# Masks added on VectorE, 1 / rms spread over the columns through HBM in three stages, FoX values in thirds, and squares of the embedding moved to later places

## Chip, cores, metric

The kernel runs on one core of a Trainium2 chip. The metric is the device time of one execution in microseconds (us), taken as a median of several executions. TensorE (PE) multiplies matrices into PSUM; VectorE (DVE), ScalarE (ACT) and GpSimd (POOL) do the elementwise work; SyncE (SP) issues most transfers. DVE and ACT can read PSUM. Each engine has its own stream of instructions, done in order.

## Reference

The reference is a trunk of two layers with 256 tokens of 1024 elements, all in float32. Cut to what matters:

```python
for i in range(2):
    x = x + 0.5 * swiglu(rms_norm(x, g), w_in, w_out)     # FFN, hidden size 2816
    x = x + mixer(rms_norm(x, g))                         # layer 0: MLA, layer 1: FoX
    x = x + 0.5 * swiglu(rms_norm(x, g), w_in, w_out)     # FFN
    x = x + gated embedding of p[i], gate from rms_norm(x, g)
out = rms_norm(x, g)

def attention:                                            # 8 heads, blocks of 128 queries
    s = where(allowed, scores, -1e30)
    o = softmax(s) @ v
# MLA: allowed = key's chunk of 64 <= query's chunk
# FoX: allowed = key <= query, and s += cum[query] - cum[key]; its projection gives q, k, v and 8 gates
```

The layers' order, and with it the names used below: FFN 0, MLA, FFN 1, embedding 0, FFN 2, FoX, FFN 3, embedding 1.

## The kernel before

**Precision and weights.** Every large product takes float32 as two parts, high and low, and does three matmuls: high by high, high by low, low by high. Activations lie with features on the 128 partitions and tokens on 256 columns (a token has 1024 features, so 8 blocks, `KD`), each block as a pair; one matmul against high weights takes both parts of a block at once (512 columns, L236), a second one against low weights takes the high part (256 columns, L237). The class `Weights` (L63 to 139) runs a plan of all weight tiles in order of use. A fetch on SP's queue brings a tile of 512 KB into `raw` (four buffers, L90), ACT copies it rounded into `whi` (L99), and DVE subtracts to get `wlo` (L103); there are seven buffers of such pairs. `pump` does the next tile's DVE step and issues the next fetch, `get` takes tiles for use, and `catch_up` pumps when fewer than some number lie ahead.

**Order.** The order in the code is the order on each engine: there is no scheduler. PSUM has seven banks in rotation and an eighth for small tiles.

**Norms.** The class `Norm` (L262 to 320) collects what the next stage needs while this one ends: `high` writes the gain times x, rounded (ACT at L276, or DVE at L274), `low` the rest (DVE, L281), `square` a square on ACT (L287), which POOL adds to `acc` (L292). The division by the rms is done behind the next stage's product: `by_token` (L301 to 311) sums `acc` over partitions by two matmuls into `pst`, DVE makes the mean `v` (L309), and POOL the power −1/2, `rtok`, with a token on each partition, 128x2 (L311). `by_column` (L313 to 320) spreads it to 256 columns on every partition: two matmuls with `rtok` broadcast against the identity (four records, L316) and an ACT copy, `rb` (L319).

**FFN** (L323 to 414). Each of 22 chunks of the hidden layer has a gate bank `pg` and an up bank `pu`. A bank ends as `two` = bank times `rb` (DVE, L330), `gu` (POOL), a sigmoid-weighted product over ACT and POOL, and `hs`, the split result (ACT L213, DVE L217). The first pair of banks (`blocks`, L253) is begun without the last feature block, so that this block's `high` and `low` may come late: first blocks 0 to 6 of every bank, then block 7. Then comes chunk 1's gate with `by_token`, and its up with `by_column`.

**Attention** (L417 to 556). For a head, `scores` (L424) has TensorE fill `psc`, where one bank holds 128 queries by 128 keys and 128 queries by 256 keys; the mask comes in as a matmul of the identity against a table of 0 and a very negative number (`masked`, L558 to 564, 8 in MLA, 8 in FoX); DVE reduces the two maxima (L428, L429) and makes the bias `nm` (L432 or L438); ACT takes the exponential of `psc` with its sum `den` (L441, L442). `shares` divides, TensorE turns the shares into `pt` (L456), ACT copies them to `ptS` (L458), and `po` is the product with the values (L463, L464). Weight products of later heads and of the output lie between these as fillers.

**FoX values** (L746 to 775). The projection to 1024 value columns and 8 gate columns runs in four chunks: 264, 256, 256 and 256 columns, each with 8 blocks, 2 halves of the tokens and 3 matmuls (L221 to L223), `pv`. `by_token` stands in chunk 0, `by_column` in chunk 1.

**Embedding 0** (`ple`, L814 to 855). For each of 8 feature blocks d: product `ps`, `zg` = `ps` times `rb` (DVE, L818), sigmoid `sg` (ACT, L819), `low` of block d − 1, a pump, `ge` = embedding times `sg` (L827), `state` += `ge` (L828), then `high` and `square` of block d for FFN 2's norm.

**Start** (L964 to 996). The first weights and x come as eight pieces (`lead0`, `lead1`) on SP's queue; TensorE does 18 matmuls on zeros (`cold`, L983) until the first piece is there.

Of the kernel before, what the change touches and what calls it, by code (L numbers as in the profile page):

```python
# [11 lines left out]
F32 = mybir.dt.float32  # L12
# [7 lines left out]
P = 128  # L20
# [20 lines left out]
GAINS = 80  # L41

# [100 lines left out]
def trunk(ctx, tc, xT, xt, pT, pos, freq, bf, lead0, lead1, ffn_in, ffn_out, w_down, w_uq, w_ukv, mla_o,  # L143
          fox_qk, fox_v, fox_f, fox_o, ple_gate, ple_proj, ple_rows, gain_row, out):
# [6 lines left out]
    psum = ctx.enter_context(tc.tile_pool(name="psum", bufs=7, space=bass.MemoryType.PSUM))  # L151
    psm = ctx.enter_context(tc.tile_pool(name="psm", bufs=1, space=bass.MemoryType.PSUM))
# [23 lines left out]
    plan.extend(fox_f[c] for c in range(2))  # L176
    plan.extend(fox_v[c] for c in range(KD - 2))
# [4 lines left out]
    plan.extend(ple_rows[c, k] for c in range(2) for k in range(KD // 2))  # L182

# [69 lines left out]
    def blocks(ps, x):  # L253

        ws = W.get(len(ps))
        for ks in (range(KD - 1), range(KD - 1, KD)):
            for p, w in zip(ps, ws):
                part(p, w, x, ks, KD - 1)
        W.done(*ws)


    class Norm:  # L262
# [50 lines left out]
        def by_column(self):  # L313
            pb = psm.tile([P, T], F32, name="pb", tag="small")
            for t in range(2):
                nc.tensor.matmul(pb[:, t * P:(t + 1) * P], self.rtok[:, t:t + 1].to_broadcast([P, P]), ident,  # L316
                                 start=True, stop=True)
            self.rb = work.tile([P, T], F32, name="rb", bufs=3)
            nc.scalar.activation(self.rb, pb, AF.Copy)  # L319
            self.rb2 = self.rb.rearrange("p (o t) -> p o t", o=1).to_broadcast([P, 2, T])  # L320


    def ffn(norm, nxt, then=None, first=None, meanwhile=None, later=None):  # L323
# [35 lines left out]
        if first:  # L359
            waits.append((bank("pg"), bank("pu")))  # L360
            first([p for ps in waits for p in ps])
        else:
            blocks(waits[0], norm.pair)
            W.pump(2)
        at = len(waits)
        for c in range(at, KF):
            pg = bank("pg")
            block(pg, norm.pair)
            if c == at:
                if not first:  # L370
# [12 lines left out]
            up(c, pu, c > at)  # L383
# [33 lines left out]
    def attention(project, score, v, scale, nxt, lag, fills, early, cumq=None):  # L417
# [6 lines left out]
        def scores(h):  # L424
            ps = bank("psc", (P, 3 * P))
            score(h, (ps[:, :P], ps[:, P:]), ps.rearrange("p (a b) -> p a b", b=P)[:, 0::2, :])
            m = work.tile([P, 2], F32, name="m", bufs=3)
            nc.vector.reduce_max(m[:, 0:1], ps[:, :P], axis=AX.X)  # L428
            nc.vector.reduce_max(m[:, 1:2], ps[:, P:], axis=AX.X)  # L429
            nm = work.tile([P, 2], F32, name="nm", bufs=3)  # L430
            if cumq is None:
                nc.vector.scalar_tensor_tensor(nm, m, -1.0, scale, op0=ALU.mult, op1=ALU.mult)  # L432
# [6 lines left out]
            pr = work.tile([P, 3 * P], F32, name="pr", bufs=4)  # L439
            den = work.tile([P, 2], F32, name="den", bufs=3)  # L440
            nc.scalar.activation(pr[:, :P], ps[:, :P], AF.Exp, bias=nm[:, 0:1], scale=by[0], accum_out=den[:, 0:1])  # L441
            nc.scalar.activation(pr[:, P:], ps[:, P:], AF.Exp, bias=nm[:, 1:2], scale=by[1], accum_out=den[:, 1:2])  # L442
            probs[h] = pr, den
# [113 lines left out]

    def masked(diagonal, i):  # L558


        a = slice(0 if i else P // 2, P)
        n = a.stop - a.start
        nc.tensor.matmul(diagonal[:, :, a], identb, cmask[:, i:i + 1, a].to_broadcast([P, 2, n]), start=False,
                         stop=False)
# [7 lines left out]
    def mla(norm, nxt):  # L572
# [111 lines left out]
        def score(h, dst, diagonal):  # L684
            for t in range(2):
                nc.tensor.matmul(dst[t], qT[:, h, t * P:(t + 1) * P], kT[:, h, :(t + 1) * P], start=t == 0, stop=False)
            masked(diagonal, 0)
            for t in range(2):
                nc.tensor.matmul(dst[t], qr[:, h, t * P:(t + 1) * P], kr[:, h % 2, :(t + 1) * P], start=False,
                                 stop=t == 1)  # L690

        attention(project, score, v, qscale, nxt, 3, MLA_FILLS, 4)


    def fox(norm, nxt):
# [50 lines left out]
        for c in range(4):  # L746
            w = W.get(2)
            n = T + H if c == 0 else T
            pv = [bank("pv0", (P, n)), bank("pv1", (P, n))]
            for k in range(KD):  # L750
                for t in range(2):
                    a = (k % 4) * n
                    mm3(pv[t], [norm.pair[:, k, u, t * P:(t + 1) * P] for u in range(2)],
                        [u[:, a:a + n] for u in w[k // 4][1:]], k == 0, k == KD - 1)
                if (c, k) == (0, KD - 2):
                    norm.by_token()
                elif (c, k) == (1, 3):
                    norm.by_column()
                elif (c, k) == (2, 2):
                    steps = gates()  # L760
                if steps:
                    next(steps, None)
                if k % 4 == 3:
                    W.done(w[k // 4])
                    if k == 3:
                        W.pump()
                        W.catch_up()
            for t in range(2):
                r = norm.rtok[:, t:t + 1]
                if c == 0:  # L770
                    nc.scalar.activation(zt[:, t, :].rearrange("p (j i) -> p j i", i=32)[:, :, :H],
                                         pv[t][:, T:].rearrange("p (o h) -> p o h", o=1).to_broadcast([P, 3, H]),
                                         AF.Copy, scale=r)
                nc.scalar.activation(v[:, t, c * T:(c + 1) * T], pv[t][:, :T], AF.Copy, scale=r)
            W.pump()
# [12 lines left out]
        def score(h, dst, diagonal):  # L788
# [3 lines left out]
            masked(diagonal, 1)  # L792
# [4 lines left out]
        attention(project, score, v, FOX_SCALE, nxt, 2, FOX_FILLS, 4, cumq=cumq)  # L797
# [16 lines left out]
    def ple(pp, norm, nxt):  # L814
        def gated(d, z, e):
# [4 lines left out]
            if d:  # L820
                nxt.low(d - 1, hT[:, d - 1, :])
# [141 lines left out]

    ROW = T + 4 * P  # L964
    lead = big.tile([P, 2 * KD + KD * ROW + 2 * D], F32, name="lead", tag="big")
# [3 lines left out]
    nc.sync.dma_start(lead[:, :2 * KD + ROW], lead0)  # L969
# [12 lines left out]
    for _ in range(18):  # L982
        nc.tensor.matmul(cold, warm[:, :P], warm, start=True, stop=True)  # L983
# [39 lines left out]
    identb = const.tile([P, P], BF16, name="identb")  # L1023
    cmask = const.tile([P, 2, P], BF16, name="cmask")
# [7 lines left out]
    def tables():  # L1032
# [6 lines left out]
        nc.vector.tensor_copy(identb, ident)  # L1039
        yield  # L1040
        nc.gpsimd.memset(cmask, 0.0)
        nc.gpsimd.memset(cmask[:64, 0, 64:], NEG)
        nc.gpsimd.affine_select(out=cmask[:, 1, :], in_=cmask[:, 1, :], compare_op=ALU.is_ge, fill=NEG, base=0,
# [94 lines left out]
    for i in range(2):  # L1138
# [8 lines left out]
        if i == 0:  # L1147
            n0, n1 = Norm(G_FFN + 16, KD, D), Norm(G_MIX + 8, KD, D)
            ple(p.pair, n3, n0)
            ffn(n0, n1, AF.Exp)  # L1150
        else:
            ple_by_token(p.pair, n3)
# [8 lines left out]
def _layout(x, p, positions, ffn_norm, ffn_w_in, ffn_w_out, mix_norm, mla_w_down, mla_q_norm, mla_w_uq,  # L1161
# [41 lines left out]

    v = w[:, 2 * hd + T:3 * hd].reshape(2, KD // 2, P, 3, T)
    a["fox_v"] = np.ascontiguousarray(v.transpose(3, 0, 2, 1, 4)).reshape(KD - 2, P, D)
    f = np.concatenate([w[:, 2 * hd:2 * hd + T], w[:, 3 * hd:]], axis=1).reshape(2, KD // 2, P, T + H)
    a["fox_f"] = np.ascontiguousarray(f.transpose(0, 2, 1, 3)).reshape(2, P, -1)
# [11 lines left out]
          "fox_qk", "fox_v", "fox_f", "fox_o", "ple_gate", "ple_proj",  # L1219
# [21 lines left out]
```

## Time and profile before

| | us |
|---|---|
| median of 3 runs | 999.35 (998.24 to 999.6) |
| the profiled execution | 998.72 |
| its span | 996.9 |
| busy: DVE, ACT, POOL | 740.9, 514.8, 422.7 |
| granted TensorE clock | 0.998 |

The profile takes one execution; its span runs from the first to the last recorded instruction. Records of TensorE overlap, since matmuls are pipelined, so that what a matmul costs is read from one start to the next. A row of the timeline has its start, its duration, the engine, the line, the operation, its tiles and shapes, and, in brackets, the idle time of the engine before it with what ended it. A row of the groups has the busy time of all, the mean of one in ns, and the idle time before them.

### The profile page before, as it was taken

How to read it: one execution, taken by the hardware profiler on the slowest of the kernel's cores; microseconds unless marked ns; L12 is line 12 of the kernel's file. 1: busy time of each engine (PE TensorE's matmuls, PEld its weight loads, DVE VectorE, ACT ScalarE, POOL GpSimd, SP SyncE). 2: the span in 40 equal slices, each digit the busy share in tenths (PEclk: the TensorE clock that was granted, in tenths of full speed). 3: DMA queues.
4: the chain of work that ended last, by engine and by line, in shares of the span. 5: the costliest groups of instructions: out<-in, count | busy, mean ns of one | idle time of the engine just before them, and what ended most of it. 6: DMA issues, size and time to landing. Idle time of an engine off the chain costs nothing.

```text
span 996.9 us, 16021 instructions
## 1 busy us (share of the span) xinstructions
PE 986.3 (99%) x5916; PEld 872.4 (88%) x5916; DVE 740.9 (74%) x1057; ACT 514.8 (52%) x821; POOL 422.7 (42%) x348
## 2 busy tenths in 40 slices
PE   9999999999999999999999999999999999999996
PEld 7888888998988888889888888899889888888885
DVE  6777879676878877667778786666777778786664
ACT  7555444465555444446555444447445554444552
POOL 0777730110377675111477773120211477761110
PEclk9999999999999999999999999999999999999999
DMA  8576666563456566665466656655443566566561
GB/s 326 181 254 211 189 180 193 169 201 97 139 178 205 184 186 177 202 198 170 148 206 200 189 182 179 194 194 200 149 148 99 178 210 194 189 179 203 178 208 43
DMA packets 53118, 182.27 MB, mean 183 GB/s; under 512 B 6192, under 2 KB 7600, under 8 KB 52912
## 3 DMA queue, kind: packets, MB, share of 16 engines
q1 hardware_dynamic: 52608, 180.53, 57.8%
q8 instruction: 47, 0.77, 0.3%
q10 hardware_dynamic: 432, 0.72, 0.3%
q14 instruction: 31, 0.25, 0.1%
HBM read 179.00 MB, written 1.05 MB: 181 GB/s over the span
## 4 chain that ended last, share of the span: by engine, by line
PE 95%; DVE 2%; ACT 1%; issue 1%; DMA 1%; SPq 0%; POOLq 0%; POOL 0%; DVEq 0%; ACTq 0%
PE po L236 16%; PE pu L236 16%; PE pg L236 16%; PE po L237 8%; PE pu L237 8%; PE pg L237 8%; PE ps L236 5%; PE ps L237 2%; PE ps L221 2%; PE ps L223 2%; PE ps L222 2%; PE pv L221 1%; PE pv L223 1%; PE pv L222 1%; PE po L463 1%
## 5 line engine op out<-in xcount | busy, mean ns | idle before, releaser
L103 DVE TENSOR_TENSOR wlo<-raw,whi 128x1024 fp32r<-128x1024 f32 (+2 forms) x338 | 415.6, 1238 | 15.4 <-ACT whi L99 15.1
L99 ACT ACTIVATE whi<-raw 128x1024 fp32r<-128x1024 f32 (+2 forms) x338 | 335.5, 1025 | 21.9 <-DMA raw<-in_ffn_in_dram 12.4
L332 POOL TENSOR_TENSOR gu<-two 128x256 f32<-128x256 f32 x176 | 235.3, 1338 | 120.4 <-DVE two L330 111.0
L236 PE MATMUL pg<-u,whi 128*128 128x512 f32 x702 | 251.1, 395 | 0.7 <-DVE u L281 0.7
L236 PE MATMUL pu<-u,whi 128*128 128x512 f32 x702 | 250.7, 395 | 0.0
L236 PE MATMUL po<-hs,whi 128*128 128x512 f32 x704 | 246.8, 394 | 0.0
L237 PE MATMUL po<-hs,wlo 128*128 128x256 f32 x704 | 198.0, 281 | 0.0
L237 PE MATMUL pg<-u,wlo 128*128 128x256 f32 x702 | 197.5, 281 | 0.2 <-DVE wlo L217 0.2
L237 PE MATMUL pu<-u,wlo 128*128 128x256 f32 x702 | 197.3, 281 | 0.0
L236 PEld LDWEIGHTS pg<-u,whi 128*128 128x128 f32 x702 | 131.9, 188 | 31.7 <-DVE u L281 0.8
L236 PEld LDWEIGHTS po<-hs,whi 128*128 128x128 f32 x704 | 132.2, 188 | 30.9
L236 PEld LDWEIGHTS pu<-u,whi 128*128 128x128 f32 x702 | 131.9, 188 | 30.6
L237 PEld LDWEIGHTS pg<-u,wlo 128*128 128x128 f32 x702 | 132.1, 188 | 0.8 <-DVE wlo L217 0.5
L237 PEld LDWEIGHTS po<-hs,wlo 128*128 128x128 f32 x704 | 132.5, 188 | 0.0
L237 PEld LDWEIGHTS pu<-u,wlo 128*128 128x128 f32 x702 | 132.2, 188 | 0.0
L292 POOL TENSOR_TENSOR acc<-acc,sq 128x256 f32<-128x256 f32 x42 | 46.1, 1098 | 172.6 <-ACT sq L287 151.1
L213 ACT ACTIVATE hs<-hid 128x256 fp32r<-128x256 f32 x88 | 36.8, 418 | 143.0 <-POOL hid L350 140.9
L350 POOL TENSOR_TENSOR hid<-sg,gu 128x256 f32<-128x256 f32 x88 | 105.4, 1198 | 6.9
L217 DVE TENSOR_TENSOR hs<-hid,hs 128x256 fp32r<-128x256 f32 x88 | 63.4, 721 | 48.6 <-ACT hs L213 48.6
L330 DVE TENSOR_TENSOR two<-pg,rb 128x512 f32<-128x512 f32 x88 | 60.3, 685 | 47.0 <-PE pg L237 39.7
L276 ACT ACTIVATE u<-state 128x256 fp32r<-128x256 f32 x47 | 24.0, 510 | 123.8 <-DVE state L397 104.6
L344 ACT ACTIVATE sg<-gu 128x256 f32<-128x256 f32 x88 | 36.8, 418 | 79.1 <-POOL gu L332 79.1
(261 smaller groups left out, 1185.5 us busy)
## 6 DMA issues: line engine op xcount, KB each, us to landing
raw<-in_ffn_in_dram SPq DMA_DIRECT2D x172, 512.0 KB, 3.7
raw<-in_ffn_out_dram SPq DMA_DIRECT2D x64, 512.0 KB, 4.1
raw<-in_ffn_out_dram SPq DMA_DIRECT2D x32, 384.0 KB, 3.6
raw<-in_fox_qk_dram SPq DMA_DIRECT2D x16, 512.0 KB, 3.6
raw<-in_mla_o_dram SPq DMA_DIRECT2D x8, 512.0 KB, 5.0
raw<-in_ple_gate_dram SPq DMA_DIRECT2D x8, 512.0 KB, 4.8
raw<-in_fox_o_dram SPq DMA_DIRECT2D x8, 512.0 KB, 3.4
raw<-in_ple_rows_dram SPq DMA_DIRECT2D x8, 512.0 KB, 4.1
```

Source lines behind the costliest of these rows:

```text
L99: self.nc.scalar.activation(self.pairs[i][0][:, c], self.raws[i][:, c], AF.Copy)
L103: self.nc.vector.tensor_sub(lo[:, c], self.raws[i][:, c], hi[:, c].bitcast(F32))
L213: nc.scalar.activation(hi, src, AF.Copy)
L217: nc.vector.tensor_sub(lo, src, hi.bitcast(F32))
L221: nc.tensor.matmul(ps, w[0], x[0], start=first, stop=False)
L236: nc.tensor.matmul(ps, hi, x[:, k], start=k == 0, stop=False)
L237: nc.tensor.matmul(ps[:, 1, :], lo, x[:, k, 0, :], start=False, stop=k == last)
L292: nc.gpsimd.tensor_add(new, self.acc, sq)
L330: nc.vector.tensor_mul(two, ps, norm.rb2)
L332: nc.gpsimd.tensor_add(gu[c, i], two[:, 0, :], two[:, 1, :])
L344: nc.scalar.activation(sg, gu.pop((c, 0)), AF.Silu)
L350: nc.gpsimd.tensor_mul(hid[c], gu.pop((c, 0)), gu.pop((c, 1)))
```

## The change

Six parts; the mathematics stays.

1. *Masks.* The 16 mask matmuls, `masked` and the bf16 identity go. `cmask` is now 128x2x256 with zeros on the left half. One DVE instruction per block of keys adds the mask to the scores, writes the result to `pr` in SBUF and gives the maximum; the exponentials read `pr`.

2. *Spreading.* `spread()` writes `rtok` to a row of 256 elements in HBM by one transfer and reads the row back to all 128 partitions by a second one, both on SP's queue. FFN 1, FoX and FFN 3 use it in place of `by_column`. In the two FFNs `by_token` moves forward too, to behind the first pair of banks and one pump; in FoX to (0, 5), with the spread at (0, 7). FFN 2 keeps the old way (`soon=False`), and FFN 0 and the embeddings do.

3. *`blocks`* takes three passes: blocks 0 to 5, then 6, then 7.

4. *FoX values.* Three chunks of 344 columns, the gate columns first; 9 weight tiles instead of 8.

5. *Embedding 0.* The square of block d − 1 comes behind the sigmoid of block d; the squares of blocks 7, 5 and 6 come at the end.

6. *Start.* The first piece of the lead is issued ahead of all, cut in two: 528 columns on SP's queue, 256 on ACT's. 16 matmuls on zeros instead of 18.

```diff
+    nc.sync.dma_start(lead[:, :a], lead0[:, :a])
+    nc.scalar.dma_start(lead[:, a:b], lead0[:, a:])
...
-        for ks in (range(KD - 1), range(KD - 1, KD)):
+        for ks in (range(KD - 2), range(KD - 2, KD - 1), range(KD - 1, KD)):
...
+        def spread(self):
+            row = dram.tile([1, T], F32, name="row", bufs=4)
+            nc.sync.dma_start(row.rearrange("o (t p) -> p (o t)", p=P), self.rtok)
+            self.rb = work.tile([P, T], F32, name="rb", bufs=3)
+            nc.sync.dma_start(self.rb, row.to_broadcast([P, T]))
+            self.both()
...
             blocks(waits[0], norm.pair)
-            W.pump(2)
+            W.pump()
+            if soon:
+                norm.by_token()
+                norm.spread()
+            W.pump()
...
             if c == at:
-                norm.by_column()
+                if first or not soon:
+                    norm.by_column()
...
-            score(h, (ps[:, :P], ps[:, P:]), ps.rearrange("p (a b) -> p a b", b=P)[:, 0::2, :])
+            score(h, (ps[:, :P], ps[:, P:]))
             m = work.tile([P, 2], F32, name="m", bufs=3)
-            nc.vector.reduce_max(m[:, 0:1], ps[:, :P], axis=AX.X)
-            nc.vector.reduce_max(m[:, 1:2], ps[:, P:], axis=AX.X)
+            pr = work.tile([P, 3 * P], F32, name="pr", bufs=4)
+            for i, a in enumerate((slice(0, P), slice(P, 3 * P))):
+                nc.vector.tensor_tensor_reduce(pr[:, a], ps[:, a], mask[:, P - i * P:], 1.0, NEG, op0=ALU.add,
+                                               op1=ALU.max, accum_out=m[:, i:i + 1])
...
-            nc.scalar.activation(pr[:, :P], ps[:, :P], AF.Exp, bias=nm[:, 0:1], scale=by[0], accum_out=den[:, 0:1])
-            nc.scalar.activation(pr[:, P:], ps[:, P:], AF.Exp, bias=nm[:, 1:2], scale=by[1], accum_out=den[:, 1:2])
+            nc.scalar.activation(pr[:, :P], pr[:, :P], AF.Exp, bias=nm[:, 0:1], scale=by[0], accum_out=den[:, 0:1])
+            nc.scalar.activation(pr[:, P:], pr[:, P:], AF.Exp, bias=nm[:, 1:2], scale=by[1], accum_out=den[:, 1:2])
...
-            masked(diagonal, 0)
...
-        for c in range(4):
-            w = W.get(2)
-            n = T + H if c == 0 else T
+        for c in range(3):
+            pv = [bank("pv0", (P, FV)), bank("pv1", (P, FV))]
...
-                elif (c, k) == (1, 3):
-                    norm.by_column()
+                elif (c, k) == (0, 7):
+                    norm.spread()
...
             if d:
+                if d < KD - 2:
+                    nxt.square(hT[:, d - 1, :])
                 nxt.low(d - 1, hT[:, d - 1, :])
...
             if d < KD - 1:
                 nxt.high(d, src)
-                nxt.square(src)
             else:
-                nxt.last(d, src)
+                nxt.high(d, src, True)
+                nxt.low(d, src)
+                for b in (d, d - 2, d - 1):
+                    nxt.square(hT[:, b, :])
...
-    for _ in range(18):
+    for _ in range(16):
```

How this stands in the engines' orders is shown at three places. First SP's queue at the start of FFN 1, after the change (`raw` are fetches of weights; `rtok`, `row` and `rb` as above):

```order
L92 DMA raw_3031<-in_ffn_in_dram 128x1024
L92 DMA raw_3073<-in_ffn_in_dram 128x1024
L337 DMA row_3082<-rtok_3080 128x2x1
L339 DMA rb_3084<-row_3082 128x256
L92 DMA raw_3090<-in_ffn_in_dram 128x1024
```

Before, the fetches follow one another there without a break; now a write of 1 KB to HBM and a broadcast read of 128 KB stand between two of them, and the write needs `rtok`. On DVE, the `v` ahead of `rtok` now stands behind the third of four `wlo` there; before, it stood behind the fourth and waited for `pst` behind the next gate's product.

Second, DVE in MLA's softmax, from the end of one head's product (`os`) over the next head's scores; before:

```order
L217 TENSOR_TENSOR os_2452<-po_2651,os_2452 128x256
L428 TENSOR_REDUCE m_2675<-psc_2669 128x1
L429 TENSOR_REDUCE m_2675<-psc_2669 128x1
L432 SCALAR_TENSOR_TENSOR nm_2678<-m_2675,qscale_2434 128x2
L103 TENSOR_TENSOR wlo_2667<-raw_2445,whi_2666 128x1024
L448 RECIPROCAL inv_2699<-den_2681 128x2
```

and after (an ISA row with two outputs is the combined instruction, one with `m` alone the read of its accumulator):

```order
L229 TENSOR_TENSOR os_2451<-po_2645,os_2451 128x256
L459 ISA pr_2669,m_2668<-psc_2663,cmask_174 128x128
L459 ISA m_2668 128x1
L459 ISA pr_2669,m_2668<-psc_2663,cmask_174 128x256
L459 ISA m_2668 128x1
L463 SCALAR_TENSOR_TENSOR nm_2672<-m_2668,qscale_2433 128x2
L105 TENSOR_TENSOR wlo_2661<-raw_2444,whi_2660 128x1024
L478 RECIPROCAL inv_2692<-den_2674 128x2
```

Each reduction has become two instructions, ahead of `nm`, on which the exponentials hang.

Third, ACT at the end of embedding 0, from the sigmoid of block 5; before:

```order
L819 ACTIVATE sg_5268<-zg_5267 128x256
L99 ACTIVATE whi_5273<-raw_5071 128x1024
L276 ACTIVATE u_4948<-state_78 128x256
L287 ACTIVATE sq_5282<-state_78 128x256
L819 ACTIVATE sg_5312<-zg_5311 128x256
L99 ACTIVATE whi_5317<-raw_5077 128x1024
L276 ACTIVATE u_4948<-state_78 128x256
L287 ACTIVATE sq_5326<-state_78 128x256
L819 ACTIVATE sg_5356<-zg_5355 128x256
L287 ACTIVATE sq_5365<-state_78 128x256
```

and after:

```order
L839 ACTIVATE sg_5254<-zg_5253 128x256
L299 ACTIVATE sq_5258<-state_83 128x256
L101 ACTIVATE whi_5263<-raw_5061 128x1024
L288 ACTIVATE u_4938<-state_83 128x256
L839 ACTIVATE sg_5298<-zg_5297 128x256
L101 ACTIVATE whi_5303<-raw_5067 128x1024
L288 ACTIVATE u_4938<-state_83 128x256
L839 ACTIVATE sg_5338<-zg_5337 128x256
L299 ACTIVATE sq_5347<-state_83 128x256
L299 ACTIVATE sq_5351<-state_83 128x256
L299 ACTIVATE sq_5355<-state_83 128x256
```

A square no longer stands between `u` (the `high` of a block) and the sigmoid of the next one; the last three stand together behind the last sigmoid, still ahead of the next weight tile.

More of the change, by code (lines that the diff above doesn't have):

```diff
@@ L175, in trunk @@
     plan_ffn(2)
-    plan.extend(fox_f[c] for c in range(2))
-    plan.extend(fox_v[c] for c in range(KD - 2))
+    plan.extend(fox_v[c, :, a * FV:min(a + 3, KD) * FV] for c in range(3) for a in range(0, KD, 3))
     plan.extend(fox_qk[c] for c in range(2 * H))
@@ L369, in ffn @@
             if c == at:
-                if not first:
+                if not (first or soon):
                     norm.by_token()
@@ L556, in attention @@
             finish(d)
[L558 to L564, printed above, removed]
     def keys_values():
@@ L690, in score @@
                                  stop=t == 1)
-        attention(project, score, v, qscale, nxt, 3, MLA_FILLS, 4)
+        attention(project, score, v, cmask[:, 0, :], qscale, nxt, 3, MLA_FILLS, 4)
     def fox(norm, nxt):
@@ L1020, in first @@
                 n0.by_token()
-    identb = const.tile([P, P], BF16, name="identb")
-    cmask = const.tile([P, 2, P], BF16, name="cmask")
+    cmask = const.tile([P, 2, 2 * P], BF16, name="cmask")
     bf_sb = const.tile([G, 1], F32, name="bf_sb")
```

65 lines of the change are left out of this document (32 added, 33 removed).

## The prediction

> **What bounds the kernel now.** I read the page first: its span, its first part, and its chain of work that ended last.
>
> ```profile
> span 996.9 us, 16021 instructions
> PE 986.3 (99%) x5916; PEld 872.4 (88%) x5916; DVE 740.9 (74%) x1057; ACT 514.8 (52%) x821; POOL 422.7 (42%) x348
> PE 95%; DVE 2%; ACT 1%; issue 1%; DMA 1%; SPq 0%; POOLq 0%; POOL 0%; DVEq 0%; ACTq 0%
> ```
>
> TensorE is never long without work and carries 95% of the chain. So an edit is worth the TensorE time that it removes, or the gap that it opens or closes there; work on the other engines counts only if it makes TensorE wait. The waits that end on TensorE, the next view, are small (waited-for place, us, times, longest):
>
> ```profile
> PE pg L236 <- DVE u L281: 0.7, 2, 0.5
> PE po L463 <- ACT ptS L458: 0.2, 1, 0.2
> ```
>
> No edit can win much by ending a wait: the whole stake is a few us in 998.72, the profiled execution's time, of which 996.9 are the span and 1.8 lie around it. That execution stands 0.63 under the median of the runs, 999.35. All sums are made on the profiled one and carried over with that difference.
>
> **The change, part by part.** Prices on TensorE are distances from one start to the next in its timeline, because its records overlap (start, duration).
>
> *Masks.* Rows of an MLA head and of a FoX head:
>
> ```profile
> 215.84 0.22 PE L563 MATMUL psc<-cmask,identb 128*128 128x128 bf16 x1
> 215.90 0.87 PE L689 MATMUL psc<-kqv 128*128 128x128 f32 x4
> 698.74 0.27 PE L563 MATMUL psc<-cmask,identb 128*128 128x256 bf16 x1
> 698.84 0.33 PE L794 MATMUL psc<-drop,pick 96*128 96x128 bf16 x2
> ```
>
> A mask matmul takes 0.06 in MLA and 0.10 to 0.11 in FoX: eight each, 0.5 and 0.87. In FoX I count −0.87. In MLA the masked scores come back through a tight loop, so the 0.5 belongs to the next sum.
>
> *MLA softmax.* The loop of DVE and ACT for one head (the last TENSOR_REDUCE of the scores, ACT's first exponential, the read of its sum, the second one, and the reciprocal that waits for it):
>
> ```profile
> 227.04 0.41 DVE L429 TENSOR_REDUCE m<-psc 128x1 f32<-128x256 f32 x1
> 227.77 0.46 ACT L441 ACTIVATE pr<-psc,nm,qscale 128x128 f32<-128x128 f32 x1 [1.72 <-DVE nm L432]
> 228.12 0.19 ACT L441 ACTIVATION_READ_ACCUMULATOR pr<-psc,nm,qscale 128x1 f32 x1
> 228.22 0.56 ACT L442 ACTIVATE pr<-psc,nm,qscale 128x256 f32<-128x256 f32 x1
> 228.90 0.17 DVE L448 RECIPROCAL inv<-den 128x2 f32<-128x2 f32 x1 [0.58 <-ACT pr L442]
> ```
>
> DVE and ACT wait for each other in turn here, so time added to the loop adds to its period. The combined instruction (add, maximum, copy) replaces a TENSOR_REDUCE over the same elements, and each gets a 128x1 read of its accumulator behind it. The trace has no such read on DVE; ACT's takes one start slot of 0.10 (228.12 to 228.22), DVE's own small record 0.17. Two reads per head: 0.2, bounds 0 (an overlapped read and a combined pass as fast as the reduce) and 0.5 (two slots of 0.17 and a pass slower by a third of the 0.41). I take 0.2, as ACT's is the same operation. The exponentials now read SBUF, not PSUM; two groups of ACT's table, a conversion that reads SBUF and one that reads PSUM, show the nearest price:
>
> ```profile
> L213 ACT ACTIVATE hs<-hid 128x256 fp32r<-128x256 f32 x88 | 36.8, 418 | 143.0 <-POOL hid L350 140.9
> L465 ACT ACTIVATE os<-po 128x256 fp32r<-128x256 f32 x16 | 6.1, 382 | 6.6 <-PE po L464 6.6
> ```
>
> 418 against 382 ns: +0.04, or +0.07 for both. TensorE is late by what three heads accumulate before fillers cover it (the third head's po already waits 0.2 in the second view): 3 × 0.27 = +0.81; of the mask matmuls only the three ahead of it shorten the way, −0.17. MLA: +0.64, bounds −0.4 (all masks gained, no slower loop) and +1.6.
>
> *1 / rms in three stages.* Rows of the old spreading by TensorE in FFN 1, then the same stage's power, load and later tolerance:
>
> ```profile
> 274.25 0.61 PE L316 MATMUL pb<-ident,rtok 128*128 128x128 f32 x4
> 274.61 0.47 PE L236 MATMUL pg<-u,whi 128*128 128x512 f32 x1
> 274.93 0.27 PE L237 MATMUL pg<-u,wlo 128*128 128x256 f32 x1
> ```
>
> The pb matmuls take 0.36 and the next matmul 0.32, not the 0.23 that the rows of psv below show: 0.46 a stage, −1.38 in three. In FoX rb is needed only behind v, of whose three chunks two, 15 us by the sum below, are left when it is issued, so −0.46 stands there. In the two FFNs the first product waits for rb at once:
>
> ```profile
> 267.90 2.35 DVE L103 TENSOR_TENSOR wlo<-raw,whi 128x1024 fp32r<-128x1024 f32 x2
> 271.79 1.62 POOL L311 TENSOR_TENSOR rtok<-v,mhalf 128x2 f32<-128x2 f32 x1 [6.03 <-DVE v L309]
> 275.31 0.69 DVE L330 TENSOR_TENSOR two<-pg,rb 128x512 f32<-128x512 f32 x1 [2.45 <-ACT rb L319]
> raw<-in_ffn_in_dram SPq DMA_DIRECT2D x1, 512.0 KB, 5.3
> fr<-in_freq_dram SPq DMA_DIRECT2D x1, 0.5 KB, 3.1
> pos_i<-in_pos_dram SPq DMA_DIRECT2D x1, 128.0 KB, 4.4
> out_dram<-fin SPq DMA_DIRECT2D x2, 256.0 KB, 2.3
> ```
>
> After the change v stands behind the third of four wlo (about 269.1, half of the 2.35 on), the power ends at 269.1 + 0.16 for v + 1.62 = 270.9, and the first transfer is issued then. The fetch ahead of it on the same queue (raw, issued at 269.1) lands 5.3 later, at 274.4; the 1 KB behind it at 274.4 to 274.9, where an idle queue would give 270.9 + 2.3 = 273.2, as the stores to HBM do. The broadcast takes 3.1 by the smallest read, 4.4 by the only other broadcast; I take 3.1. So rb is there at 277.9, 2.6 after the 275.3 of before; bounds 276.3 and 279.3, 1.0 and 4.0 late. DVE stands at that product, and wlo of later tiles behind it. The least tolerance is here:
>
> ```profile
> 284.85 1.21 DVE L103 TENSOR_TENSOR wlo<-raw,whi 128x1024 fp32r<-128x1024 f32 x1
> 288.92 0.28 PE L237 MATMUL pu<-u,wlo 128*128 128x256 f32 x1
> ```
>
> That wlo ends at 286.06, 2.86 ahead of its matmul, and 2.4 ahead once TensorE is earlier by 0.46. A stall is then 2.6 − 2.4 = 0.2. FFN 3 is the same code; 0.2 is a narrow remainder of two larger numbers, and for the second place I allow 0.5: +0.7 in all, bounds 0 and 3.2 (twice 4.0 − 2.4). SP issues its next fetch only behind both, some 4 us late; the pairs of weights have seven buffers, so the tile that it brings is not due for far longer.
>
> *Trainium skill.* In "DMA: Bandwidth & Descriptors", section "Anatomy of one DMA", the Trainium skill puts a fixed part of about 2.0 us into a transfer, most of it the receipt of the write, heaviest for HBM. That fits the 2.3 of the stores; 0.5 KB at 3.1 does not fit. By it, as an estimate, rb would come at 274.9, both stalls would go and the sum would be 0.7 lower. Its section "Queues, rings and completion order" speaks against the change: each engine takes a queue's descriptors in ring order, so the 1 KB stands behind the fetch, as the 5.3 lets one suspect.
>
> *Late squares and blocks in three passes.* The gap at the start of the FFN behind the embedding (TensorE, then the two ACT records ahead of the sigmoid):
>
> ```profile
> 480.13 0.28 PE L237 MATMUL pg<-u,wlo 128*128 128x256 f32 x1
> 480.90 0.50 PE L236 MATMUL pg<-u,whi 128*128 128x512 f32 x1 [0.49 <-DVE u L281]
> 481.24 0.28 PE L237 MATMUL pg<-u,wlo 128*128 128x256 f32 x1
> 484.48 0.39 PE L236 MATMUL pg<-u,whi 128*128 128x512 f32 x1
> 484.89 0.39 PE L237 MATMUL pg<-u,wlo 128*128 128x256 f32 x1
> 480.23 0.40 ACT L287 ACTIVATE sq<-state 128x256 f32<-128x256 f32 x1
> 480.54 0.40 ACT L819 ACTIVATE sg<-zg 128x256 f32<-128x256 f32 x1
> ```
>
> Against normal distances of 0.12 and 0.23 the starts lose 0.65 (480.13 to 480.90) + 0.11 (to 481.24) and 0.18 (484.48 to 484.89): 0.94. The square takes 0.31 ahead of the sigmoid on which the next block hangs; behind it, each block is that much shorter, so u of the last two blocks comes earlier, and the third pass lets TensorE work on other chunks until it does. I take −0.9; bounds −0.94 and −0.1, if something else in the block (the product on DVE) holds the chain.
>
> *FoX values.* Start distances by width:
>
> ```profile
> 212.60 0.40 PE L222 MATMUL psv<-whi,kv 128*128 128x512 f32 x1
> 212.84 0.40 PE L223 MATMUL psv<-wlo,kv 128*128 128x512 f32 x1
> 684.95 0.28 PE L221 MATMUL pv<-whi,u 128*128 128x256 f32 x1
> 685.07 0.28 PE L222 MATMUL pv<-whi,u 128*128 128x256 f32 x1
> ```
>
> 0.12 for 256 columns and 0.235 for 512; 344 lie 0.34 of the way, 0.158. 144 × 0.158 = 22.7 against 192 × 0.12 = 23.0: −0.3, bounds 0 and −0.9 (144 distances that fall by the ratio of the columns, were 0.115 a floor).
>
> *Start.* TensorE becomes dense when the third piece of the lead lands:
>
> ```profile
> 7.20 0.51 ACT L276 ACTIVATE u<-lead 128x256 fp32r<-128x256 f32 x1 [1.26 <-DMA lead<-in_lead_dram]
> ```
>
> The change issues the first piece earlier and on two queues, but the bytes ahead of the third are the same, and the first matmuls behind the warming ones, now two fewer, would reach the same wait earlier. −0.1, bounds −0.9 and +0.5. The Trainium skill ("Trainium Kernel Development and Optimization", section "Key Constraints") says that transfers of several queues share the same 16 engines and that only issue time is saved; by it the sum would be the same.
>
> **Sum**: −0.87 + 0.64 − 1.38 + 0.7 − 0.9 − 0.3 − 0.1 = −2.2; 998.72 − 2.2 = 996.5, and 999.35 − 2.2 = **997.1** as a median.
>
> **Rivals.**
> 1. *The transfers come late (the other side: slower).* Place: rb in FFN 1 and 3. For it: a fetch of 5.3 in front, 4.4 for a broadcast. Against: the idle-queue prices. Every us past 277.7 costs one in each stage. The gain of 2.9 without stalls is spent when both lose 1.45 (rb at 279.2); with both transfers at 4.4 behind the fetch, rb is at 283.2, 7.9 late, 5.5 a stage: 999.35 − 2.9 + 11.0 = 1007.4. Midway, 3 a stage, gives 1002.4.
> 2. *The transfers are quick and the loop pays nothing.* No stalls, MLA −0.4, half of the start's bound: −0.7 − 1.04 − 0.4 leads to 995.0. For it: 2.3 for a store; against: the read of 0.5 KB at 3.1.
> 3. *The squares don't do it.* If DVE's product holds the embedding's chain, −0.1 instead of −0.9: 997.9. MLA at its bound of +1.6 gives 998.1, the same answer.
>
> **Chances.** Forecast 0.44, rival 1 0.16, rival 2 0.22, rival 3 0.18. The forecast's own range is 996 to 998.5 (its larger bounds on one side at a time); the range goes to rival 2 below and to the start of rival 1 above, 994.5 to 1000.4. A measurement of this kernel tells 0.2%, 2.0 us, from no change: faster means under 997.35. The forecast lies half on each side (0.27 faster, 0.17 same), rival 2 is faster, rival 3 same, rival 1 same (0.06) or slower (0.10). Faster 0.49, same 0.41, slower 0.10.
>
> **What would show it.** In the profile after: rb landing some 7 us behind the end of the power's record, with DVE's product waiting for a DMA and a TensorE wait on wlo in FFN 1 and 3 of 0.2 to 0.5; a loop of MLA that is longer by 0.27 a head; distances of 0.158 in v; no gap at 480. The prediction is wrong if a TensorE wait over 1 us stands in an FFN, if MLA is no longer than before, or if the gap at the start moves.

## Result and profile after

The changed kernel takes 1011.89 us (median of 4 runs, 1010.45 to 1015.16) against 998.8 us (998.15 to 999.6) of the kernel before: 1.4% slower, ratio 1.0137, 95% interval 1.0118 to 1.0155. The profiled execution of the change took 1010.45, of which 1008.6 are the span: 11.7 more than before. The forecast was 997.1, with a range of 994.5 to 1000.4.

Of the page of the change, the span, the busy times, the granted TensorE clock over 40 slices, and the chain that ended last:

```profile
span 1008.6 us, 15913 instructions
PE 988.1 (98%) x5838; PEld 871.8 (86%) x5838; DVE 735.9 (73%) x1089; ACT 513.9 (51%) x817; POOL 424.0 (42%) x348
PEclk9999999999989999999999999999999899999999
PE 86%; DVE 5%; DMA 5%; ACT 2%; issue 1%; POOL 0%; SPq 0%; POOLq 0%; ACTq 0%; DVEq 0%
```

TensorE's busy time is about that of before, so the time was added beside its work. Transfers, not in the chain before beyond 1%, now hold 5% of it, and two slices show a lower clock. Cutting the span at the first product of each stage in TensorE's timeline says where (us; `no_spread` is an experiment below):

| stage | before | after | no_spread |
|---|---|---|---|
| start and FFN 0 | 191.14 | 191.31 | 191.02 |
| MLA | 71.44 | 70.65 | 70.28 |
| FFN 1, gate and up | 124.31 | 131.55 | 124.27 |
| FFN 1 out, embedding 0 | 91.25 | 91.12 | 91.10 |
| FFN 2, gate and up | 125.39 | 124.26 | 124.26 |
| FFN 2 out | 61.68 | 61.64 | 61.63 |
| FoX | 107.57 | 107.24 | 106.43 |
| FFN 3, gate and up | 124.30 | 131.30 | 124.28 |
| FFN 3 out, embedding 1, end | 99.86 | 99.57 | 99.50 |

FFN 1 and FFN 3, the two FFNs with the new spreading, lose 7.24 and 7.00. All else together gains 2.5. TensorE's waits say what ended the stalls:

```profile
PE pu L248 <- DVE two L353: 5.8, 2, 3.0
PE pu L249 <- DVE wlo L105: 4.0, 2, 2.0
PE cold L1005 <- DVE warm L1002: 1.1, 1, 1.1
PE psc L811 <- DVE kqv L805: 1.0, 1, 1.0
```

Each FFN waits twice: 3 us for a PSUM bank (`pu` cannot start before DVE has emptied an older bank into `two`) and 2 us for weights. Behind both stands `rb`. SP's queue at FFN 1, then DVE's and TensorE's timelines:

```profile
266.26 2.60 SPq L92 DMA_DIRECT2D raw<-in_ffn_in_dram  x3
270.29 0.39 SPq L337 DMA_DIRECT2D row<-rtok  x1
278.74 0.34 SPq L339 DMA_DIRECT2D rb<-row  x1
```

```profile
284.34 0.69 DVE L353 TENSOR_TENSOR two<-pg,rb 128x512 f32<-128x512 f32 x1 [12.06 <-DMA rb<-row]
```

```profile
281.91 0.28 PE L249 MATMUL pg<-u,wlo 128*128 128x256 f32 x1
285.18 0.47 PE L248 MATMUL pu<-u,whi 128*128 128x512 f32 x1 [2.99 <-DVE two L353]
287.67 0.58 PE L249 MATMUL pu<-u,wlo 128*128 128x256 f32 x1 [2.02 <-DVE wlo L105]
288.04 0.63 PE L248 MATMUL pu<-u,whi 128*128 128x512 f32 x1
```

The broadcast waits for the row, so the row's 1 KB took 8.45 from its issue (270.29) to 278.74; the broadcast took 5.6 more, to 284.34. DVE stood 12 us. TensorE's last rows are also slower themselves: 0.63 for a matmul of 512 columns that takes 0.39 elsewhere. A row of the window view has a stretch, its length, the busy times of PE, PEld, DVE, ACT and POOL, the granted clock, and the DMA engines' share and GB/s:

```profile
282.00:285.20 3.20, 0.21 (x3) 0.05 (x1) 0.86 (x2) 0.00 (x0) 0.09 (x1) 1.00 0.97 270
285.20:288.00 2.80, 0.78 (x2) 0.47 (x3) 2.41 (x3) 1.36 (x2) 2.72 (x3) 0.59 0.24 99
288.00:292.00 4.00, 4.00 (x14) 3.42 (x14) 3.05 (x4) 1.78 (x3) 2.89 (x4) 0.50 0.42 131
292.00:298.00 6.00, 6.00 (x34) 5.22 (x34) 4.12 (x6) 3.15 (x5) 4.89 (x5) 0.95 0.58 174
```

The clock that is missing, 0.41 of 2.8, 0.5 of 4.0 and 0.05 of 6.0, adds up to 3.45 us, which is some 6.9 us at half clock, behind a wait of 3.0. The Trainium skill, "TensorE: Matmul & The Clock Gate", "Part 1: The HAM clock gate", has a gate that halves the clock after an idle window of about 3.4 us and decides by such windows: two of them are 6.8, which agrees, but here a wait of 3.0 was enough.

### The profile page after: what moved, and what is told of

Read it like the earlier page. It is cut to its first block, busy times and chain, and to the rows that moved or that the text cites. A ratio compares the mean times of both kernels' runs of the same rounds, so it can differ in the third digit from the quotient of the medians.

```text
span 1008.6 us, 15913 instructions
## 1 busy us (share of the span) xinstructions
PE 988.1 (98%) x5838; PEld 871.8 (86%) x5838; DVE 735.9 (73%) x1089; ACT 513.9 (51%) x817; POOL 424.0 (42%) x348
## 4 chain that ended last, share of the span: by engine, by line
PE 86%; DVE 5%; DMA 5%; ACT 2%; issue 1%; POOL 0%; SPq 0%; POOLq 0%; ACTq 0%; DVEq 0%
PE po L248 16%; PE pu L248 15%; PE pg L248 15%; PE po L249 8%; PE pu L249 8%; PE pg L249 7%; PE ps L248 4%; DVE wlo L105 2%; PE ps L249 2%; DMA row<-rtok 2%; PE ps L235 1%; PE ps L234 1%; PE ps L233 1%; DMA rb<-row 1%; DMA raw<-in_fox_qk_dram 1%
## 5 line engine op out<-in xcount | busy, mean ns | idle before, releaser
L355 POOL TENSOR_TENSOR gu<-two 128x256 f32<-128x256 f32 x176 | 227.5, 1294 | 139.0 <-DVE two L353 129.5
L248 PE MATMUL pu<-u,whi 128*128 128x512 f32 x702 | 254.8, 399 | 5.8 <-DVE two L353 5.8
L373 POOL TENSOR_TENSOR hid<-sg,gu 128x256 f32<-128x256 f32 x88 | 113.6, 1291 | 6.9
L229 DVE TENSOR_TENSOR hs<-hid,hs 128x256 fp32r<-128x256 f32 x88 | 59.2, 672 | 58.5 <-ACT hs L225 58.5
```

The source lines that it names most:

```text
L229: nc.vector.tensor_sub(lo, src, hi.bitcast(F32))
L248: nc.tensor.matmul(ps, hi, x[:, k], start=k == 0, stop=False)
L355: nc.gpsimd.tensor_add(gu[c, i], two[:, 0, :], two[:, 1, :])
L373: nc.gpsimd.tensor_mul(hid[c], gu.pop((c, 0)), gu.pop((c, 1)))
```

## Experiments

Each run's time stands beside runs of the kernel before in the same job (998.2 to 999.1). Stage lengths are those of the profiled execution.

### Where the loss is

**ffn_column**: the old spreading back in FFN 1 and FFN 3, FoX as in the change.

```diff
-        ffn(n2, n3, AF.Sigmoid, later=p)
+        ffn(n2, n3, AF.Sigmoid, later=p, soon=False)
```

> The changed kernel with FFN 1 and FFN 3 spreading by TensorE again, at the old place; FoX keeps its transfers. Theory A (the two transfers take 14 us, TensorE runs out of banks and then of weights, and its clock is halved for 6.8 us): FFN 1 and 3 lose 7.2 and 7.0 us only for that, so 1011.9 - 14.2 = 997.7, and no granted clock under 1.0 behind a stall. Rival B (the loss comes from another part that FFN 1 and 3 share, such as the blocks in three passes): the time stays over 1005.

994.79 us, ratio 0.9958 (0.9943 to 0.9973): FFN 1 and 3 take 124.27 and 124.28, and no clock under 1.0 stands behind a stall. B falls. From profiled execution to profiled execution the fall is 14.4, near A's 14.2; the medians are further apart, as the change's lies 1.4 above its profiled execution and this run's 1.2 below.

**before_spread**: the opposite, only that spreading (with its earlier `by_token`) added to the kernel before.

```diff
...
             blocks(waits[0], norm.pair)
-            W.pump(2)
+            W.pump()
+            if soon:
+                norm.by_token()
+                norm.spread()
+            W.pump()
...
```

> The kernel before with only the spreading through HBM in FFN 1 and FFN 3 (and by_token moved forward there), all else as before. Theory A: +7.2 and +7.0, so 998.8 + 14.2 = 1013. Rival B: within 3 us of 998.8.

1011.06 us, ratio 1.012 (1.0105 to 1.0135): +12.2. FFN 1 and 3 lose 6.2 and 7.2. The spreading alone is enough, and its loss is about that of the whole change.

**kept_warm**: TensorE given idle work in the first wait.

```diff
+            if c == 3 and soon and not first:
+                busy = psm.tile([P, T], F32, name="busy", tag="small")
+                for _ in range(28):
+                    nc.tensor.matmul(busy, warm[:, :P], warm, start=True, stop=True)
             pu = bank("pu")
```

> The changed kernel with 28 matmuls on zeros (some 3.1 us) ahead of the up product of chunk 3 in FFN 1 to 3's new stages (FFN 1 and 3), where TensorE stood 3.15 us. They fill the first wait and add no work of use. Theory A1 (the idle time of over 3 us is what halves the clock, and that costs about 2 us a stage beyond the waits): the granted clock stays at 1.0 and the time falls by 3 to 5 us to about 1008. Rival A2 (the half clock lies where weights were awaited anyway): clock at 1.0, time within 1 us of 1011.9. Rival A3 (the clock falls for another reason, the second wait of 2.3 us included): clock as in the changed kernel, time unchanged.

1007.72 us (1007.38 to 1007.76), 4.2 less than the change, and the same stretches at full clock:

```profile
282.00:285.20 3.20, 3.20 (x31) 2.83 (x29) 1.51 (x3) 0.00 (x0) 0.74 (x2) 1.00 0.89 309
285.20:288.00 2.80, 1.31 (x8) 0.91 (x8) 1.76 (x2) 1.78 (x3) 2.72 (x3) 1.00 0.19 59
288.00:292.00 4.00, 2.90 (x17) 2.29 (x17) 3.07 (x4) 1.65 (x3) 2.90 (x4) 1.00 0.39 125
```

Without the idle time the clock stays up: A3 falls. The two stages themselves gain only 1.04 and 1.17; with the clock up, TensorE waits for weights again (2.90 busy of 4.00). And `rb` came earlier here, in FFN 1 at:

```profile
283.69 0.69 DVE L353 TENSOR_TENSOR two<-pg,rb 128x512 f32<-128x512 f32 x1 [11.34 <-DMA rb<-row]
```

That is 21.70 behind the stage's start (261.99), against 22.38 in the change. A stage loses about one us for each that `rb` is late (see the section on the prediction), so 0.68 of the 1.04 goes with quicker transfers; in FFN 3 it is 0.91 of the 1.17 (21.33 against 22.24). Some 0.3 a stage is left for the clock: the time fell as A1 had it, but not for A1's reason, and A2 is nearer in cause, though not in time. The largest share of the clock that the runs show is 1.0, in before_spread, whose FFN 3 had `rb` as late as its FFN 1 but was at half clock for 6.8 us, not 3.4. Of the other 2.0 of the 4.2, 0.9 lies in stages of the profiled executions where nothing was changed, and 1.1 in how far the medians lie above those executions; both stay open.

### Why the row takes 8.4 us

**whole_row**: the power on one partition, so that the row is one piece of 1 KB.

```diff
...
+            nc.tensor.matmul(pst, ones[:, :1], self.acc, start=True, stop=True)
...
+            nc.gpsimd.tensor_tensor(r, v, mhalf[:1, :1].to_broadcast([1, T]), op=ALU.pow)
...
+            nc.sync.dma_start(row, r)
...
```

> The changed kernel, where in FFN 1 and 3 the power is taken on one partition, 256 elements in a row (one matmul of ones against the sum, DVE and POOL on 1x256), so that the row goes to HBM as one piece of 1 KB instead of 256 pieces of 4 bytes; the broadcast is as in the change. Theory C1 (the 256 pieces make the 8.4 us from issue to landing): the row takes 2.3 to 3 us, rb comes about 6 us earlier, stalls of at most 1 us a stage and no half clock: 998 to 1000. Rival C2 (any write to HBM that is read back takes it): the row keeps about 8 us and the time stays at 1010 to 1014.

1074.2 us, 62 slower than the change, and not for the transfer. POOL's power, then SP's two transfers:

```profile
269.30 42.05 POOL L348 TENSOR_TENSOR vrow<-vrow,mhalf 1x256 f32<-1x256 f32 x1 [3.76 <-DVE vrow L346]
```

```profile
311.37 0.25 SPq L350 DMA_DIRECT2D row<-vrow  x1
312.48 0.34 SPq L352 DMA_DIRECT2D rb<-row  x1
```

The power over 256 columns takes 42 us, over two columns of 128 partitions 1.6. As a test of the time it failed, but it shows the row in one piece: 1.1 us. (The broadcast behind it took 4.7, to DVE's product at 317.23.) **row_turned** has that row without the slow power.

```diff
...
+            for t in range(2):
+                nc.tensor.matmul(pb[:, t * P:(t + 1) * P], self.rtok[:, t:t + 1], ident, start=True, stop=True)
+            nc.scalar.activation(r, pb, AF.Copy)
...
+            nc.sync.dma_start(row, r)
...
```

> The changed kernel, where in FFN 1 and 3 two matmuls against the identity turn rtok into one row of 256 elements on one partition, behind the gate product of chunk 1, and ACT copies it; the row then goes to HBM as one piece of 1 KB (1.1 us from its issue to that of the broadcast in the run whole_row, 8.4 in the changed kernel) and comes back by the same broadcast (4.8 to 5.6). It costs the TensorE time that the change saved. Theory C1 (the time lies in the 256 pieces of 4 bytes, and a tolerance of some 2.4 us is real): rb at about 277.5 in FFN 1, no bank wait, no half clock, weights late by at most 0.5 a stage: 995 to 997. Rival C2 (TensorE stalls for any transfer of rb, at whatever time): above 1003.

997.0 us, ratio 0.9985 (0.9975 to 0.9994). SP's row and broadcast, and DVE's first product:

```profile
273.66 0.25 SPq L349 DMA_DIRECT2D row<-rrow  x1
276.43 0.34 SPq L351 DMA_DIRECT2D rb<-row  x1
```

```profile
280.05 0.69 DVE L365 TENSOR_TENSOR two<-pg,rb 128x512 f32<-128x512 f32 x1 [6.26 <-DMA rb<-row]
```

The row takes 2.77, behind a fetch, and the broadcast 3.6. `rb` comes 2.5 later than I had expected, the clock stays up, and FFN 1 and 3 lose 0.8 and 0.6 against before. C2 falls: it isn't transfers as such, but how late they are.

**half_pieces**: 128 pieces of 8 bytes, columns put in order by ACT.

```diff
-            nc.sync.dma_start(row.rearrange("o (t p) -> p (o t)", p=P), self.rtok)
+            nc.sync.dma_start(row.rearrange("o (p t) -> p (o t)", t=2), self.rtok)
...
```

> The changed kernel, where the row in HBM is written as 128 pieces of 8 bytes (both halves of the tokens side by side) instead of 256 of 4 bytes, in all three stages; ACT puts the columns back in order behind the broadcast (some 0.5 us more on the way). Theory D1 (the quiet time of 5.7 us behind the last packet goes with the number of pieces): the row takes 5 to 6 us instead of 8.4, rb comes some 2.3 us earlier, and with a shorter wait the time falls to 1004 to 1008. Rival D2 (it goes with writes under some size, whatever their number, or is one fixed receipt): the row keeps 8 to 8.5 us, and the time is 1012 to 1014.

The row took 5.0 in FFN 1, as D1 has it, and 4.0 in FFN 3, less than that; SP's queue in FFN 1:

```profile
270.83 0.33 SPq L337 DMA_DIRECT2D row<-rtok  x1
275.83 0.33 SPq L340 DMA_DIRECT2D mixed<-row  x1
```

The time, 1012.82 us, lies in D2's range, but for another reason: ACT's copy stood ahead of other work in its stream. FoX waited 6.6 for `zt` behind it and lost 7.4, and in the FFNs (4.5 and 4.2 lost) weights waited for `whi`. The time speaks for neither theory; the row's time speaks for D1. In FFN 1 the clock was at half for some 3.4 us behind waits of only 1.5 and 0.8 (the stretch from 282.5 to 286.0 had 0.51).

**two_queues**: 256 pieces of 4 bytes, half by SP's queue, half by ACT's.

```diff
+            for t, q in ((0, nc.sync), (1, nc.scalar)):
+                q.dma_start(row[:, t * P:(t + 1) * P].rearrange("o p -> p o"), self.rtok[:, t:t + 1])
...
```

> The changed kernel, where the 256 pieces of 4 bytes go as two transfers of 128 pieces at once, one on SP's queue and one on ACT's, in all three stages (ACT then waits for rtok in its stream). With 128 pieces of 8 bytes the row took 5.0 and 4.0 us, with 256 of 4 bytes 8.4. Theory D3 (the pieces are worked off one by one at HBM, whatever queue they come by): the broadcast is issued 8 to 9 us after the first row transfer, time 1010 to 1014. Rival D4 (each queue's own 128 pieces set it): issued after 4 to 5 us, a stall of 2 to 3 us a stage and a shorter or no half clock: 1001 to 1006.

1008.85 us (1008.19 to 1009.57). In FFN 1 the broadcast was issued at 278.97, 8.8 behind the row's issue at 270.18. D4 falls. The time is a little below D3's range: behind the row's issue `rb` came 0.4 earlier than in the change in both FFNs, and FFN 1 and 3 took 130.83 and 130.89; the rest stays open.

**pieces_apart**: a measurement that nothing waits for, in a kernel that spreads by TensorE.

```diff
+            if apart:
+                far = dram.tile([P, 2, P], F32, name="far", bufs=1)
+                row = far[:, :, 0:1].rearrange("p t o -> p (t o)")
+            else:
+                near = dram.tile([1, T], F32, name="near", bufs=1)
+                row = near.rearrange("o (t p) -> p (o t)", p=P)
+            nc.sync.dma_start(row, self.rtok)
...
+            nc.sync.dma_start(back, row)
...
```

> no_spread with a measurement that nothing waits for: behind the spreading by TensorE, rtok is written to HBM as 256 pieces of 4 bytes and read back to a small tile, in FFN 1 with the pieces 512 bytes apart, in FFN 3 side by side as in the change. The distance from the write's issue to that of the read back is the write's time. Theory H1 (pieces that fall into the same stretch of HBM wait for one another): 2 to 4 us apart, about 8 us side by side. Theory H2 (256 separate writes take it wherever they fall): about 8 us both times.

```profile
273.15 0.61 SPq L349 DMA_DIRECT2D far<-rtok  x1
277.13 0.57 SPq L351 DMA_DIRECT2D back<-far  x1
...
780.80 0.39 SPq L349 DMA_DIRECT2D near<-rtok  x1
789.55 0.37 SPq L351 DMA_DIRECT2D back<-near  x1
```

The same 256 pieces of 4 bytes take 4.0 us with 512 bytes between them (FFN 1) and 8.75 side by side (FFN 3), in one execution (995.09 us) each; the change has 8.45 and 8.46 in these two FFNs, so the FFN isn't the reason. H1's numbers hold: about half of the 8.4 goes with pieces that lie side by side in one KB of HBM, by whatever queue they come. How they hold one another up isn't shown. In the change the row's packets are over at 272.9, and until the row has landed the DMA engines move nothing (share and GB/s at the end):

```profile
272.90:278.70 5.80, 5.80 (x35) 5.10 (x34) 0.00 (x0) 1.42 (x2) 0.00 (x0) 1.00 0.00 0
```

The Trainium skill, "DMA: Bandwidth & Descriptors", "Specifications", names read-modify-write below 512 bytes; that would be such a reason, but no run here shows the mechanism. Its fixed part of about 2.0 us ("Anatomy of one DMA", given there for GpSimd's path, not for SP's) is near the row in one piece (1.1 alone, 2.4 and 2.8 behind a fetch), not near this one: the measurement decides.

### The other parts

**no_spread**: no transfer of 1 / rms at all; FoX spreads by TensorE at (1, 2).

```diff
-                elif (c, k) == (0, 7):
-                    norm.spread()
+                elif (c, k) == (1, 2):
+                    norm.by_column()
...
```

> The changed kernel without any transfer of 1 / rms: FFN 1, FFN 3 and FoX spread by TensorE (FoX in chunk 1 of its values). Against ffn_column (994.8), which keeps the transfers in FoX: theory E1 (FoX's transfers hold SP's queue for 9.5 us, weights come late, and that costs the wait of 1.0 for kqv of the changed kernel in some executions): between 0.7 faster and the same, 994.1 to 994.8, without a wait on kqv. Rival E2 (in FoX the transfers are hidden and the two matmuls cost 0.46): 995.3.

994.93 us, ratio 0.9964 (0.9951 to 0.9976): faster than both kernels, and level with ffn_column. FoX takes 106.43 there and 106.42 in ffn_column. E2's 0.46 isn't seen between these two, and E1's wait neither; with the same transfers FoX took 107.24 in the change (with the wait of 1.0), 106.68 in kept_warm, and 105.98 in row_turned and whole_row, 0.45 less than here. What the transfers save there, they give back in some executions.

**masks_undone**: no_spread with the masks by TensorE.

```diff
-                nc.vector.tensor_tensor_reduce(pr[:, a], ps[:, a], mask[:, P - i * P:], 1.0, NEG, op0=ALU.add,
-                                               op1=ALU.max, accum_out=m[:, i:i + 1])
+            nc.vector.reduce_max(m[:, 0:1], ps[:, :P], axis=AX.X)
+            nc.vector.reduce_max(m[:, 1:2], ps[:, P:], axis=AX.X)
...
+            masked(diagonal, 0)
...
```

> no_spread with the masks by TensorE again (table, 16 matmuls, two plain reductions, exponentials from PSUM). Theory F1 (the combined instruction costs DVE little, so that MLA gains most of its 0.5 and FoX its 0.87): MLA's stage is longer by 0.6 to 1.0 than in no_spread, FoX by 0.8 to 0.9, the whole 1.4 to 1.9 slower. Theory F2 (the record's own: MLA pays 0.64 for the longer loop): MLA shorter by 0.6, the whole 0.2 slower.

996.45 us (995.99 to 997.02), 1.5 slower: F1's size. FoX is longer by 0.97, MLA by 0.29, which is less than F1 has. DVE's rows in no_spread show why F2 falls:

```profile
226.09 0.28 DVE L459 CUSTOM_DVE_ANT_0 pr<-psc,cmask 128x128 f32<-128x128 f32 x1
226.29 0.08 DVE L459 DVE_READ_ACCUMULATOR2_ANT m<- 128x1 f32 x1
226.29 0.42 DVE L459 CUSTOM_DVE_ANT_0 pr<-psc,cmask 128x256 f32<-128x256 f32 x1
226.64 0.08 DVE L459 DVE_READ_ACCUMULATOR2_ANT m<- 128x1 f32 x1
226.75 0.16 DVE L463 SCALAR_TENSOR_TENSOR nm<-m,qscale 128x2 f32<-128x2 f32 x1
```

The first read starts where the next combined instruction starts: it takes no time of its own. From the first combined instruction to `nm` are 0.66, and 0.64 with plain reductions (226.89 to 227.53 in masks_undone). The period of the loop, from one reciprocal to the next, is 3.12, and 3.05 there.

**squares_undone** and **blocks_undone**: no_spread with one of the two parts at embedding 0 taken back.

```diff
-                if d < KD - 2:
-                    nxt.square(hT[:, d - 1, :])
...
-                for b in (d, d - 2, d - 1):
-                    nxt.square(hT[:, b, :])
```

```diff
-        for ks in (range(KD - 2), range(KD - 2, KD - 1), range(KD - 1, KD)):
+        for ks in (range(KD - 1), range(KD - 1, KD)):
```

> no_spread with embedding 0's squares at their old places. The stage of FFN 2 was 1.13 shorter in every run with the change. Theory G1 (the record's: the square ahead of the sigmoid made the chain late): FFN 2 loses 0.6 to 1.0 of that again and TensorE waits for u there. Theory G2 (the third pass of blocks alone covers it): FFN 2 as in no_spread, within 0.1.

> no_spread with blocks in two passes (blocks 0 to 6, then 7). Theory G1: FFN 2 loses at most 0.3, as the chain itself is early enough. Theory G2: FFN 2 loses 0.6 to 1.0 and TensorE waits for u.

One timed execution each (997.28 and 995.6 us), read by stages. FFN 2 takes 125.40 with the squares at their old places, as before the change, and 124.23 with blocks in two passes, as with three. G1 holds in the time: the squares are the whole gain of 1.13. It doesn't in the wait: in squares_undone TensorE's waits have 0.5 for `wlo` there, not for `u` as before the change.

## Why the prediction was wrong

The step that failed is the first transfer: "the 1 KB behind it at 274.4 to 274.9", from stores to HBM that took 2.3. Those are 256 KB in long pieces; the row is 256 pieces of 4 bytes in one KB, and took 8.45. I bounded a transfer by its bytes and by its place in the queue, and the trace of before holds no write in such pieces. The second size, 3.1 for the broadcast, was off too: 5.6, beyond the 4.4 of `pos_i`. That was not the only other broadcast, as I wrote: `fin<-in_gain_row_dram`, 512 KB, is one too, and the trace of before has it at 5.4. Together rb came 14.0 behind the row's issue, not 7.0, and the stalls that stood in the sum with +0.7 cost 14.2. Against the stage's start it came 9.65 later than before (284.34 − 261.96, against 275.31 − 262.58), not 2.6.

From there the working holds in size. A delay less a tolerance of 2.4 gives 7.25 for 9.65 late; the stage lost 7.24, or 7.7 with the 0.46 saved. row_turned, 3.6 late (280.05 − 263.70 = 16.35 against 12.73), lost 0.8 where 1.2 would be due; whole_row, 42.2 late, lost 39.7 where 39.8 would; kept_warm, 9.0 late and never at half clock in that stage, lost 6.2 where 6.6 would. So the delay sets the price. But what made it up wasn't as written: I named late weights alone, while seven PSUM banks ran out first, and then the clock was halved, which added little (some 0.3 a stage). The rival "the transfers come late" had the place, most of the delay (7.9) and of the price (5.5 a stage, 1007.4 in all); I gave it 0.16, and kept its end out of the range.

- *MLA*: +0.64 forecast, a gain of 0.79 measured. The term of the accumulator reads, 0.2 a head, is 0.02, since they overlap; the loop grew by 0.07 a head, not 0.27. The stage varies with the same code of MLA by more than this (70.2 to 71.4, with a wait of 1.1 of `pt` for `pr` in the longer ones), so the masks' part is only bounded by the loop. It isn't the gain: masks_undone, with TensorE's masks, has 70.57, 0.87 less than before. What shortened MLA stays open.
- *Masks in FoX*: −0.87 forecast, 0.97 measured.
- *FoX spreading*: −0.46 "hidden" is half right. SP's queue stood from 678.6 to 688.2 behind the row, weights came late, and `psc` waited 1.0 in the change's profile; in other executions it did not. The seven buffers of weights were too thin a cover there.
- *Embedding 0*: −0.9 forecast, −1.13 measured; I shared it between squares and the third pass, and the squares alone do it.
- *FoX values*: distances of 0.158 forecast; the rows of `pv` of the change are 0.15 to 0.16 apart. The stage in masks_undone is 0.17 shorter than before; the part wasn't tried alone.
- *Start*: −0.1 forecast. The first product comes at 4.2 to 4.5, against 4.8 before and 4.5 in before_spread, which has the old start. Start and FFN 0 together take 191.1 in those two, and 191.0 to 192.6 in the twelve traces with the new start, eleven of them longer, by 0.5 in the middle; in the longest (ffn_column) TensorE waited 1.3 for FFN 0's `rtok`. So it looks like a small loss. It wasn't tried alone and stays open.

Without any spreading by transfer the terms of the forecast make −1.5 (+0.64 − 0.87 − 0.9 − 0.3 − 0.1); no_spread gains 3.8 against its runs of before (998.69 to 994.93), the more for MLA and embedding 0.

## What to carry to other kernels

A tiny transfer is priced by its pieces and where they fall, not by its bytes: a column over 128 partitions that is written as one row of HBM was the slowest tried here, and two dependent transfers can take the place of two matmuls only where as much other work is ready as they take, here 14 us. Before a stall is priced, look how late the awaited tile is against what the buffers cover: here that gave a stage's loss within 0.7 us in every run, while the half clock, which outlasted the wait, added little. Before a run is said to show the clock's price, look whether anything else moved with it. A wait put into SP's stream holds every fetch behind it, as from 678.6 to 688.2 in FoX.

## What the runs showed of the hardware

- 256 pieces of 4 bytes to HBM, side by side: 7.8 (before_spread, FFN 3) to 9.6 us (the change, FoX) by one queue, 8.0 to 8.8 by two; 4.0 with 512 bytes between them. 128 pieces of 8 bytes: 4.0 to 5.2. One piece of 1 KB: 1.1, and 2.4 to 2.8 behind a fetch.
- The broadcast of that KB to 128 partitions took 4.8 to 5.6 behind the write of 256 pieces; behind the write in one piece 4.7 in whole_row and 3.6 to 3.7 in row_turned. Why is open.
- POOL's power takes 42 us over 256 columns of one partition and 0.7 to 1.6 over 2 columns of 128.
- The 28 matmuls of zeros in a wait of 3 us kept the clock at 1.0. Without them it stood at half for some 6.9 us behind that wait, and in half_pieces for some 3.4 us behind waits of 1.5 and 0.8.
